# Hybrid encoder block, last stage: output blocks of three rows of experts, p's split in two pieces, u's split in two halves

## The chip, the cores and the metric

The kernel runs on one core of a Trainium2 chip. The metric is device time in microseconds of one execution. The core's engines are named as the profile names them: PE (matrix products; PEld is its weight load), DVE (vector), ACT (scalar and activation functions), POOL (GpSimd), SP (issues DMAs).

## What is computed

One layer: differential attention and a short convolution, merged by gates, then a retrieval over experts ("PEER") and a norm. All is float32 with S = D = 1024. Only the last part matters here:

```python
q = (xc @ w_query).reshape(c, PEER_HEADS, 2, PEER_HALF_DIM)
...
top, pos = lax.top_k(cand, PEER_TOPK)          # 8 heads x 16 experts a token
eidx = jnp.take_along_axis(cidx, pos, axis=-1)
g = jax.nn.softmax(top, axis=-1)
u = expert_u[eidx]
a = jax.nn.gelu(jnp.einsum('chkd,cd->chk', u, xc), approximate=False)
vv = expert_v[eidx]
return jnp.einsum('chk,chkd->cd', (g.astype(a.dtype) * a), vv)
```

There are 128 x 128 experts, each a row of 1024 values of u and one of v.

## The kernel before

The eight tiles of 128 tokens are treated in two ways. Five of them (NB = 5, GB = 640 tokens) are **dense**: every expert is computed for every token, and a table of weights w_d, zero where an expert wasn't chosen, selects. Three of them (NA = 3) are **gathered**: for each of the 128 chosen experts of a token, POOL fetches 128 rows of u and v at once (`gather_gen`, L727, the indirect DMA at L741), DVE forms the dot product (L748), ACT the gelu and the weight (L750, L751), and DVE accumulates (L761). Four slots (UVT) hold fetched rows; a fetch goes out when the accumulation four before it is done.

Both run together in the last stage (L890 to L1037). Its loop (L1000) goes over i, here called **step** i: one row of 128 experts of the 128 rows (NK).

- `expert_u(i+1)` (L926): the row's u arrives transposed, as 128 x 1024, by SP's DMA in one of three buffers `raw`. `split` (L903) makes two parts of it for products at full accuracy: ACT copies the high part (L906, tile uh), DVE subtracts it for the low part (L908, tile uhl).
- `expert_z(i)` (L930): 48 matmuls of 320 columns, z = hn u, in two halves of the tokens of 24 each; `expert_u(i+1)` stands between the halves. Then ACT's gelu makes p (L942, tile pr).
- `expert_p(i)` (L945): DVE multiplies p by the weights (L946), and `split` makes ph and phl of it. 
- `expert_v(i)` (L950): v's row is loaded into `raw` and split into vh and vhl.
- `expert_out` (L962): the output, 5 tiles of tokens x 2 halves of 512 columns, is formed for a **block** of BLK = 2 rows at a time, in as many parts as the block has rows, one part a step. Four of the ten output tiles ("held", r0 to r3) stay in PSUM to the end; for the six others ("moving", m0 to m5) PE writes `pout`, of which there are two buffers, and DVE adds it into hacc (L975). The order is m0 r0 m1 r1 m2 | r2 m3 r3 m4 m5. Each tile takes 3 matmuls for each row of the block. The block before the present one is put out: step i = 2b+2 and 2b+3 put out rows 2b and 2b+1. `after`, that is `expert_p` of step i, is called at the second tile.

The buffers of a kind are counted by PHB = 4 (ph, phl), VHB = 3 (vh, vhl), and 2 for uh and uhl. A tile takes the place of the oldest of its kind, when all instructions that use that one are done.

**What sets the order.** PE and DVE run in the order of the source in this stage (`manual_schedule`, L898). ACT, POOL and SP are ordered by a planner. The gather and the selection of experts (`select_gen`, L594; for the gathered tiles, `done` is given) are generators that `tick` (L148) steps on: each group of matmuls reports its time in us (L917: columns / 2400 x 3 x number of operands), 12.8 us a step in all, and a generator moves on when its own interval has gone by. The gather's is 2.36 us while the selection runs, and 1.78 us afterwards (GATHER, L1003), with one dot product or one accumulation at a time; the selection's is 13 us (SEL_STEP_D). What they put on DVE stands in DVE's order at that place.

```python
1014              made.append(expert_z(i, us.pop(0), ahead))
1015          if b >= 0:
1016              expert_out(pv[:BLK], vv[:BLK], part, b == 0, b == NK // BLK - 1, product)
1017          product()
1018          if b >= 0 and part == BLK - 1:
1019              pv, vv = pv[BLK:], vv[BLK:]
1020          if i < NK:
1021              vv.append(expert_v(i))
```

Of the kernel before, what the change touches and what calls it, by code (L numbers as in the profile page):

```python
# [20 lines left out]
P = 128  # L21
S = 1024
D = 1024
# [21 lines left out]
UVT = 4  # L45
PHB = 4
VHB = 3
BLK = 2
NR = 2
WB = 4  # L50
WT = 32
# [3 lines left out]
SEL_STEP = 1.5  # L55
SEL_STEP_D = 13
W_STEP = 1.6
# [8 lines left out]
def block_kernel(ctx, tc, x, wqkv, wcols, wpr, wo, wq, skT, uv, uT, an_w, fn_w, fin_w, sub_w,  # L66
# [527 lines left out]
    def select_gen(small, tt, ev, gw, done=None):  # L594
# [6 lines left out]
        for a in range(2):  # L601
# [23 lines left out]
            for j in range(2):  # L625
# [5 lines left out]
                else:  # L631
# [6 lines left out]
                                op=ALU.is_equal)  # L638
                PL.tensor_tensor(out=oh, in0=oh, in1=sfv[:, :, j, :].unsqueeze(3).broadcast_to(sh), op=ALU.mult)
                V.tensor_reduce(out=ev[j][:, a * 64:(a + 1) * 64].rearrange("p (h k) -> p h k", k=TOPK),  # L640
                                in_=oh.rearrange("p h a k -> p h k a"), axis=AX.X, op=ALU.add)
# [284 lines left out]
    def expert_u(i):  # L926
        u = split(raw_rows(uT[i]), "uh", 2, [P, D], V)
        return [(u[0][:, k * P:(k + 1) * P], u[1][:, k * P:(k + 1) * P]) for k in range(KD)]

    def expert_z(i, us, mid):  # L930
        b = i // WB
        if i % WB == 0:
            wts[b] = dn.tile([P, GB // WT, WB, WT], F32, name="wt", tag="wt", bufs=2)
            SP.dma_start(out=wts[b], in_=w_d[:, :, i:i + WB, :].rearrange("c p i t -> p c i t"))
        hs = halves(GB)
        z = ps_z.tile([P, 2, 512], F32, name="z", tag="z")[:, :len(hs), :hs[0][1]]
        for j, (c0, cn) in enumerate(hs):
            passes(z[:, j, :], us, [(hh[:, k, c0:c0 + cn], hl[:, k, c0:c0 + cn]) for k in range(KD)], cn)
            if j == 0:
                mid()  # L940
        p = dn.tile([P, GB], F32, name="pr", tag="pr", bufs=1)
        A.activation(p.rearrange("p (h c) -> p h c", h=len(hs)), z, AF.Gelu)  # L942
        return p

    def expert_p(i, p):  # L945
        V.tensor_mul(p.rearrange("p (c t) -> p c t", t=WT), p.rearrange("p (c t) -> p c t", t=WT),  # L946
                     wts[i // WB][:, :, i % WB, :])
        return split(p, "ph", PHB, [P, GB], V)

# [12 lines left out]
    def expert_out(pv, vv, part, first, last, after):  # L962
        n = len(order) // BLK
        for j, (t, hf) in enumerate(order[part * n:(part + 1) * n]):
            if j == 1:
                after()
# [10 lines left out]
    def finish_rows():  # L977
# [3 lines left out]
        for t in range(NB):  # L981
# [5 lines left out]
            else:  # L987
                y = hacc[:, t - NR, :]
            A.activation(du.tile([P, D], F32R, name="uh", tag="uh", bufs=2), y, AF.Square, accum_out=ss[:, t:t + 1])
            ys.append(y)  # L990
# [7 lines left out]

    pv, vv, us = [], [], [expert_u(0)]
    for i in range(NK + BLK):  # L1000
        b, part = i // BLK - 1, i % BLK
        made = []
        gather[2] = GATHER[sel not in gens]  # L1003

        def ahead():
            if i + 1 < NK:
                us.append(expert_u(i + 1))

        def product():
            if made:  # L1010
                pv.append(expert_p(i, made.pop()))

        if i < NK:
            made.append(expert_z(i, us.pop(0), ahead))
        if b >= 0:
            expert_out(pv[:BLK], vv[:BLK], part, b == 0, b == NK // BLK - 1, product)
        product()
        if b >= 0 and part == BLK - 1:
            pv, vv = pv[BLK:], vv[BLK:]
        if i < NK:  # L1020
            vv.append(expert_v(i))
        if i == 1:
            for t in range(NR, NB):
                SP.dma_start(out=hacc[:, t - NR, :], in_=h_d[t * P:(t + 1) * P, :])
# [66 lines left out]
```

## Time and profile before

| | |
|---|---|
| median of 3 runs | 3399.04 us (3398.12 to 3399.4) |
| the profiled execution | 3390.54 us, span 3388.8 us |
| mean granted TensorE clock | 0.959 of full speed |
| busy share of the span: PE, PEld, DVE, ACT, POOL | 91%, 83%, 78%, 38%, 26% |
| last stage: first and last product of z | 1315.3 and 3343.2 us |

The span is from the first to the last instruction. A busy time counts the time in which at least one instruction of the engine runs. PE's instructions overlap, so a busy PE isn't PE at its peak. "Idle before" is the time that the engine stood still just ahead of an instruction, and "<-" names what ended it. A window's clock is the share of the full TensorE clock that was granted, 2.4 GHz being 1.00 and 1.2 GHz 0.50.

### The profile page before, as it was taken

What the parts mean: (1) busy time and instruction counts of PE and PEld (TensorE: products, weight loads), DVE (VectorE), ACT (ScalarE), POOL (GpSimd) and SP (SyncE); (2) the same over time, 40 slices, a digit from 0 to 9 for tenths busy, and PEclk for the clock granted to TensorE, in tenths of its full rate; (3) what the DMA queues carried; (4) which work ended last, traced back from release to release, by engine and by line L of the source; (5) the groups of instructions that cost most, each with busy time, mean ns of one, the idle gap of its engine ahead of it and who ended that gap; (6) DMA issues with size and microseconds to landing.
All of it is one profiled execution on the core that took longest, in us unless ns stands there. A gap on an engine that the chain in (4) does not pass through costs nothing.

```text
span 3388.8 us, 45651 instructions
## 1 busy us (share of the span) xinstructions
PE 3073.1 (91%) x17551; PEld 2804.0 (83%) x17551; DVE 2659.0 (78%) x4661; ACT 1295.8 (38%) x2341; POOL 889.2 (26%) x712
## 2 busy tenths in 40 slices
PE   8999999898989887998998998998999988999896
PEld 6799988798988787887887887887888877888785
DVE  4442564589999965988898987888988888888888
ACT  3322462446577674323223323323223332333232
POOL 2310000154353542222222222222222322223232
PEclk9999999899999998999999998999999998999999
DMA  4442223735443656777787877787777888898886
GB/s 172 156 152 73 85 87 118 248 127 212 162 176 145 230 217 240 279 268 268 273 291 262 286 267 254 278 285 254 285 282 248 325 308 303 324 324 329 293 323 247
DMA packets 237547, 801.09 MB, mean 236 GB/s; under 512 B 18832, under 2 KB 123280, under 8 KB 174096
## 3 DMA queue, kind: packets, MB, share of 16 engines
q0 software_dynamic: 64704, 442.53, 35.3%
q1 hardware_dynamic: 152592, 305.30, 26.5%
q10 hardware_dynamic: 20032, 50.34, 3.9%
q8 instruction: 138, 2.26, 0.3%
q14 instruction: 81, 0.66, 0.1%
HBM read 714.74 MB, written 83.36 MB: 236 GB/s over the span
## 4 chain that ended last, share of the span: by engine, by line
PE 26%; issue 24%; DVE 22%; DMA 11%; POOL 9%; ACT 7%; SPq 0%; POOLq 0%; ACTq 0%; DVEq 0%
POOL uvt L741 8%; DMA raw<-in_uT 6%; PE pg L228 4%; DVE acc L761 3%; DVE uvt L748 3%; PE pq L228 3%; PE z L915 3%; PE ph L228 2%; DVE hacc L975 2%; PE py L228 2%; DVE vhl L908 2%; PE pout L915 2%; PE pw L694 2%; DVE phl L908 1%; DMA uvt<-in_uv,idx 1%
## 5 line engine op out<-in xcount | busy, mean ns | idle before, releaser
L741 POOL DMA_INDIRECT uvt<-in_uv,idx x384 | 498.4, 1298 | 1498.3 <-DVE acc L761 1447.3
L915 PE MATMUL z<-actTh,uhl 128*128 128x320 f32 x2048 | 645.1, 315 | 13.6 <-DVE uhl L908 13.6
L915 PE MATMUL z<-actTh,uh 128*128 128x320 f32 x2048 | 647.4, 316 | 7.7 <-ACT pr L942 5.8
L915 PE MATMUL z<-actTl,uh 128*128 128x320 f32 x2048 | 645.5, 315 | 0.0
L748 DVE SCALAR_TENSOR_TENSOR uvt<-uvt,hng 128x1024 f32<-128x1024 f32 x384 | 467.5, 1217 | 54.2 <-DMA uvt<-in_uv,idx 26.9
L761 DVE SCALAR_TENSOR_TENSOR acc<-uvt,wt,acc 128x1024 f32<-128x1024 f32 x384 | 490.7, 1278 | 5.3 <-DMA acc<-h_d 5.0
L915 PE MATMUL pout<-vh,ph 128*128 128x512 f32 x768 | 319.0, 415 | 175.9 <-DVE hacc L975 175.8
L915 PEld LDWEIGHTS z<-actTh,uh 128*128 128x128 f32 x2048 | 398.4, 195 | 15.4 <-ACT pr L942 6.7
L915 PEld LDWEIGHTS z<-actTh,uhl 128*128 128x128 f32 x2048 | 396.8, 194 | 14.0 <-DVE uhl L908 14.0
L915 PEld LDWEIGHTS z<-actTl,uh 128*128 128x128 f32 x2048 | 397.6, 194 | 6.6
L750 ACT ACTIVATE wt<-zt 128x1 f32<-128x1 f32 x384 | 77.0, 201 | 721.3 <-DVE uvt L748 721.0
L915 PEld LDWEIGHTS pout<-vh,ph 128*128 128x128 f32 x768 | 149.0, 194 | 231.8 <-DVE hacc L975 204.5
L915 PE MATMUL pout<-vhl,ph 128*128 128x512 f32 x768 | 311.7, 406 | 1.6 <-DVE vhl L908 1.6
L915 PE MATMUL pout<-vh,phl 128*128 128x512 f32 x768 | 311.6, 406 | 0.0
L975 DVE TENSOR_TENSOR hacc<-pout,hacc 128x512 f32<-128x512 f32 x384 | 262.2, 685 | 28.9 <-PE pout L915 27.9
L717 POOL TENSOR_TENSOR o<-ms,wtr 128x512 f32<-128x512 bf16 x160 | 204.5, 1322 | 255.0 <-PE pw L694 132.4
L185 DVE TENSOR_TENSOR wl<-wr,wh 128x2048 fp32r<-128x2048 f32 x66 | 157.9, 2393 | 113.9 <-ACT wh L184 113.9
L906 ACT CAST uh<-raw 128x1024 fp32r<-128x1024 f32 x128 | 134.7, 1052 | 280.1 <-DMA raw<-in_uT 226.0
L908 DVE TENSOR_TENSOR phl<-pr,ph 128x640 fp32r<-128x640 f32 x128 | 105.6, 825 | 152.6 <-ACT ph L906 151.0
L694 PE MATMUL pw<-o,o 128*128 128x128 f32 x1280 | 172.4, 288 | 39.5 <-POOL o L717 19.1
L184 ACT CAST wh<-wr 128x2048 fp32r<-128x2048 f32 x74 | 141.0, 1907 | 164.4 <-DMA wr<-in_wq 33.2
L694 PEld LDWEIGHTS pw<-o,o 128*128 128x128 f32 x1280 | 164.2, 202 | 47.6 <-POOL o L717 24.0
(290 smaller groups left out, 6831.2 us busy)
## 6 DMA issues: line engine op xcount, KB each, us to landing
raw<-in_uT SPq DMA_DIRECT2D x128, 512.0 KB
raw<-in_uv SPq DMA_DIRECT2D x128, 512.0 KB
w_d<-wbuf ACTq DMA_DIRECT2D x20, 2048.0 KB
wt<-w_d SPq DMA_DIRECT2D x32, 1280.0 KB
wr<-in_wcols SPq DMA_DIRECT2D x28, 1024.0 KB
wr<-in_wq SPq DMA_DIRECT2D x24, 1024.0 KB
xt<-in_x SPq DMA_DIRECT2D x16, 512.0 KB
q_d<-qt POOLq DMA_DIRECT2D x32, 256.0 KB
```

The lines of the kernel that those rows point to most:

```text
L184: A.copy(out=op[0][sl], in_=src)
L185: lo.tensor_sub(op[1][sl], src, op[0][sl].bitcast(F32))
L228: PE.matmul(pd, lhsT=l[a], rhs=r[b], start=i == 0 and j == 0, stop=i == n - 1 and j == len(c) - 1)
L694: PE.matmul(pw[:, u, :], lhsT=o2[:, t + u, :], rhs=o1[:, t + u, :], start=True, stop=True)
L717: PL.tensor_tensor(out=o1.rearrange("p t i -> p i t"), in0=ms[:, 0], in1=w[:, ts].unsqueeze(1).broadcast_to(sh), op=ALU.mult)
L741: PL.indirect_dma_start(out=t[:], out_offset=None, in_=uv, in_offset=bass.IndirectOffsetOnAxis(ap=sels[c][1][:, k:k + 1], axis=0))
L748: V.scalar_tensor_tensor(u, u, 1.0, st[c], op0=ALU.mult, op1=ALU.mult, accum_out=zt)
L761: V.scalar_tensor_tensor(acc, t[:, D:2 * D], wt, acc, op0=ALU.mult, op1=ALU.add)
L906: A.copy(out=hi, in_=t)
L908: eng.tensor_sub(lo, t, hi.bitcast(F32))
L915: PE.matmul(ps, lhsT=lhs[k][a], rhs=rhs[k][b], start=first and k == 0 and j == 0, stop=last and k == n - 1 and j == 2)
L975: V.tensor_add(hacc[:, t - NR, ds], ps, hacc[:, t - NR, ds])
```

## The change

Blocks of three rows in place of two (BLK), with 5 buffers for ph and phl, 4 for vh and vhl, 3 of half the size for uh and uhl, and weights loaded for three rows at a time. Tiles are put out as m0 r0 m1 r1 | m2 r2 m3 | r3 m4 m5; the last of the 43 blocks has two rows. The split of p: product and ACT's copy at the second tile of a step's output, the subtraction at the third. The split of u: its first half after the products that use the first half of u, the second after the others; z is now formed over the halves of u, for both halves of the tokens. The selection has one more halt, between POOL's product and DVE's sum (L639, L640), and an interval of 11.6 us. The last norm's scratch tile is of another kind.

```diff
@@ -43,17 +43,17 @@
 NE = PH * TOPK
 
 UVT = 4
-PHB = 4
-VHB = 3
-BLK = 2
+PHB = 5
+VHB = 4
+BLK = 3
 NR = 2
-WB = 4
+WB = 3
 WT = 32
 WQ = 4
 WFB = 2
 GATHER = (2.36, 1.78)
 SEL_STEP = 1.5
-SEL_STEP_D = 13
+SEL_STEP_D = 11.6
 W_STEP = 1.6
 MIXW = 3
 ATT = (5, 4)
@@ -637,6 +637,8 @@
                 V.tensor_tensor(out=oh, in0=pf.unsqueeze(2).broadcast_to(sh), in1=iota_k.unsqueeze(1).broadcast_to(sh),
                                 op=ALU.is_equal)
                 PL.tensor_tensor(out=oh, in0=oh, in1=sfv[:, :, j, :].unsqueeze(3).broadcast_to(sh), op=ALU.mult)
+                if done:
+                    yield
                 V.tensor_reduce(out=ev[j][:, a * 64:(a + 1) * 64].rearrange("p (h k) -> p h k", k=TOPK),
                                 in_=oh.rearrange("p h a k -> p h k a"), axis=AX.X, op=ALU.add)
                 yield
@@ -924,20 +926,26 @@
         return t
 
     def expert_u(i):
-        u = split(raw_rows(uT[i]), "uh", 2, [P, D], V)
-        return [(u[0][:, k * P:(k + 1) * P], u[1][:, k * P:(k + 1) * P]) for k in range(KD)]
+        ur = raw_rows(uT[i])
+        for h in range(2):
+            u = split(ur[:, h * 512:(h + 1) * 512], "uh", 3, [P, 512], V)
+            us[i].append([(u[0][:, k * P:(k + 1) * P], u[1][:, k * P:(k + 1) * P]) for k in range(KD // 2)])
+            yield
 
     def expert_z(i, us, mid):
         b = i // WB
         if i % WB == 0:
             wts[b] = dn.tile([P, GB // WT, WB, WT], F32, name="wt", tag="wt", bufs=2)
-            SP.dma_start(out=wts[b], in_=w_d[:, :, i:i + WB, :].rearrange("c p i t -> p c i t"))
+            n = min(WB, NK - i)
+            SP.dma_start(out=wts[b][:, :, :n, :], in_=w_d[:, :, i:i + n, :].rearrange("c p i t -> p c i t"))
         hs = halves(GB)
         z = ps_z.tile([P, 2, 512], F32, name="z", tag="z")[:, :len(hs), :hs[0][1]]
-        for j, (c0, cn) in enumerate(hs):
-            passes(z[:, j, :], us, [(hh[:, k, c0:c0 + cn], hl[:, k, c0:c0 + cn]) for k in range(KD)], cn)
-            if j == 0:
-                mid()
+        kh = KD // 2
+        for h in range(2):
+            for j, (c0, cn) in enumerate(hs):
+                xs = [(hh[:, k, c0:c0 + cn], hl[:, k, c0:c0 + cn]) for k in range(h * kh, h * kh + kh)]
+                passes(z[:, j, :], us[h], xs, cn, h == 0, h == 1)
+            mid()
         p = dn.tile([P, GB], F32, name="pr", tag="pr", bufs=1)
         A.activation(p.rearrange("p (h c) -> p h c", h=len(hs)), z, AF.Gelu)
         return p
@@ -945,7 +953,14 @@
     def expert_p(i, p):
         V.tensor_mul(p.rearrange("p (c t) -> p c t", t=WT), p.rearrange("p (c t) -> p c t", t=WT),
                      wts[i // WB][:, :, i % WB, :])
-        return split(p, "ph", PHB, [P, GB], V)
+        hi = dv.tile([P, GB], F32R, name="ph", tag="ph", bufs=PHB)
+        A.copy(out=hi, in_=p)
+        return p, hi
+
+    def expert_lo(p, hi):
+        lo = dv.tile([P, GB], F32R, name="phl", tag="phl", bufs=PHB)
+        V.tensor_sub(lo, p, hi.bitcast(F32))
+        return hi, lo
 
     def expert_v(i):
         vr = raw_rows(uv[i * P:(i + 1) * P, D:])
@@ -960,9 +975,9 @@
                 order.append(q.pop(0))
 
     def expert_out(pv, vv, part, first, last, after):
-        n = len(order) // BLK
-        for j, (t, hf) in enumerate(order[part * n:(part + 1) * n]):
-            if j == 1:
+        cut = [-(-len(order) * j // BLK) for j in range(BLK + 1)]
+        for j, (t, hf) in enumerate(order[cut[part]:cut[part + 1]]):
+            if j in (1, 2):
                 after()
             ds = slice(hf * 512, (hf + 1) * 512)
             lhs = [(p[0][:, t * P:(t + 1) * P], p[1][:, t * P:(t + 1) * P]) for p in pv]
@@ -986,7 +1001,7 @@
                     V.tensor_add(y[:, ds], held[t][hf], y[:, ds])
             else:
                 y = hacc[:, t - NR, :]
-            A.activation(du.tile([P, D], F32R, name="uh", tag="uh", bufs=2), y, AF.Square, accum_out=ss[:, t:t + 1])
+            A.activation(dv.tile([P, D], F32R, name="vh", tag="vh", bufs=VHB), y, AF.Square, accum_out=ss[:, t:t + 1])
             ys.append(y)
         yield
         r = rstd_of(ss, D, NB, "f")
@@ -996,25 +1011,32 @@
             SP.dma_start(out=out[t * P:(t + 1) * P, :], in_=ys[t])
             yield
 
-    pv, vv, us = [], [], [expert_u(0)]
-    for i in range(NK + BLK):
+    pv, vv, us = [], [], {0: []}
+    run(expert_u(0))
+    blocks = -(-NK // BLK)
+    for i in range((blocks + 1) * BLK):
         b, part = i // BLK - 1, i % BLK
         made = []
         gather[2] = GATHER[sel not in gens]
 
+        us[i + 1] = []
+        coming = expert_u(i + 1) if i + 1 < NK else iter(())
+
         def ahead():
-            if i + 1 < NK:
-                us.append(expert_u(i + 1))
+            next(coming, None)
 
         def product():
-            if made:
-                pv.append(expert_p(i, made.pop()))
+            if made and isinstance(made[0], tuple):
+                pv.append(expert_lo(*made.pop()))
+            elif made:
+                made[0] = expert_p(i, made[0])
 
         if i < NK:
-            made.append(expert_z(i, us.pop(0), ahead))
+            made.append(expert_z(i, us.pop(i), ahead))
         if b >= 0:
-            expert_out(pv[:BLK], vv[:BLK], part, b == 0, b == NK // BLK - 1, product)
-        product()
+            expert_out(pv[:BLK], vv[:BLK], part, b == 0, b == blocks - 1, product)
+        while made:
+            product()
         if b >= 0 and part == BLK - 1:
             pv, vv = pv[BLK:], vv[BLK:]
         if i < NK:
```

## Rows read from the trace of the kernel before


**Rows 1.** Windows: length; busy of PE, PEld, DVE, ACT, POOL; clock; DMA share; GB/s.

```profile
1400.00:2550.00 1150.00, 1061.36 (x5728) 955.54 (x5727) 998.29 (x1638) 349.56 (x703) 269.87 (x208) 0.96 0.77 273
2570.00:3340.00 770.00, 686.90 (x3699) 617.93 (x3699) 665.93 (x845) 238.21 (x523) 222.78 (x168) 0.96 0.86 311
```

**Rows 2.** The groups of instructions, PE, 1400 to 2550 us.

```profile
L915 PE MATMUL z<-actTh,uh 128*128 128x320 f32 x1179 | 372.3, 316 | 2.0 <-ACT pr L942 2.0
```

**Rows 3.** The groups of instructions, PE, 2570 to 3340 us.

```profile
L915 PE MATMUL z<-actTh,uh 128*128 128x320 f32 x761 | 239.4, 315 | 0.0
```

**Rows 4.** The timeline, all engines, 2902 to 2915 us (start, duration, instruction).

```profile
2902.39 0.31 PE L915 MATMUL z<-actTh,uh 128*128 128x320 f32 x1
...
2905.96 0.33 SPq L923 DMA_DIRECT2D raw<-in_uT  x1
...
2909.47 0.40 PE L915 MATMUL pout<-vh,ph 128*128 128x512 f32 x1
...
2914.35 1.05 ACT L906 CAST uh<-raw 128x1024 fp32r<-128x1024 f32 x1 [3.97 <-DMA raw<-in_uT]
...
2914.70 0.39 PE L915 MATMUL held<-vh,phl 128*128 128x512 f32 x1
```

**Rows 5.** The waits, 1400 to 2550 us (us in total, times, longest).

```profile
PE pout L915 <- DVE hacc L975: 86.6, 37, 12.1
...
DVE phl L908 <- ACT ph L906: 78.3, 71, 3.3
...
DVE hacc L975 <- PE pout L915: 18.0, 20, 2.7
DVE pr L946 <- ACT pr L942: 17.0, 10, 5.5
DVE e L640 <- POOL sc L639: 16.6, 8, 2.1
```

**Rows 6.** The waits, 2570 to 3340 us.

```profile
DVE phl L908 <- ACT ph L906: 63.9, 47, 8.2
...
DVE uvt L748 <- DMA uvt<-in_uv,idx: 20.6, 26, 2.0
```

**Rows 7.** The timeline, DVE alone, 2881 to 2890 us.

```profile
2881.60 0.82 DVE L946 TENSOR_TENSOR pr<-pr,wt 128x640 f32<-128x640 f32 x1
2883.21 0.83 DVE L908 TENSOR_TENSOR phl<-pr,ph 128x640 fp32r<-128x640 f32 x1 [0.79 <-ACT ph L906]
2883.95 1.28 DVE L761 SCALAR_TENSOR_TENSOR acc<-uvt,wt,acc 128x1024 f32<-128x1024 f32 x1
...
2886.29 0.69 DVE L975 TENSOR_TENSOR hacc<-pout,hacc 128x512 f32<-128x512 f32 x1
2886.89 1.27 DVE L761 SCALAR_TENSOR_TENSOR acc<-uvt,wt,acc 128x1024 f32<-128x1024 f32 x1
...
2888.69 1.22 DVE L908 TENSOR_TENSOR vhl<-raw,vh 128x1024 fp32r<-128x1024 f32 x1
2889.82 1.22 DVE L748 SCALAR_TENSOR_TENSOR uvt<-uvt,hng 128x1024 f32<-128x1024 f32 x1
```

**Rows 8.** The page, the costliest groups, the whole span.

```profile
L975 DVE TENSOR_TENSOR hacc<-pout,hacc 128x512 f32<-128x512 f32 x384 | 262.2, 685 | 28.9 <-PE pout L915 27.9
```

**Rows 9.** The page, the DMA issues, the whole span.

```profile
wt<-w_d SPq DMA_DIRECT2D x32, 1280.0 KB
```

**Rows 10.** The timeline, all engines, around 2003 us.

```profile
2002.55 0.40 PE L915 MATMUL pout<-vh,phl 128*128 128x512 f32 x1
...
2002.98 1.05 ACT L906 CAST vh<-raw 128x1024 fp32r<-128x1024 f32 x1 [4.00 <-PE pout L915]
...
2005.38 1.22 DVE L908 TENSOR_TENSOR vhl<-raw,vh 128x1024 fp32r<-128x1024 f32 x1
```

**Rows 11.** The windows, a wait of PE and what follows it.

```profile
2226.00:2230.70 4.70, 0.02 (x1) 0.00 (x0) 2.83 (x5) 1.96 (x4) 0.37 (x1) 1.00 0.82 295
2230.70:2235.00 4.30, 4.28 (x15) 3.71 (x16) 4.20 (x12) 2.39 (x4) 0.57 (x1) 0.60 0.79 266
```

## The prediction

> **What bounds the kernel now.** The change touches the last stage alone, the loop over 128 rows of experts ("steps"), so I read that stage by itself. The busy table of two stretches comes first [rows 1]: one in which the selection still runs (1400 to 2550 us) and one after it (2570 to 3340 us). DVE is busy 998.3 of 1150 us and 665.9 of 770 us, and no engine is full. A step has 16 products of each kind into z, so the counts give the steps: 1179 / 16 = 73.7 in the first stretch, 15.6 us each, and 761 / 16 = 47.6 in the second, 16.2 us each [rows 2, 3]. Products alone need less: in an undisturbed round the 48 products of z take 7.08 us (2902.39 to 2909.47) and 23 output products 5.23 us (to the start of the one at 2914.70), 0.2275 us each, so 30 take 6.8 us and a step 13.9 us [rows 4]. PE's one large wait is for DVE's addition into hacc, 86.6 us in the first stretch [rows 5].
>
> DVE works 998.3 / 73.7 = 13.55 us a step and idles 2.06. Over half of its idle time has one cause: phl waits for ACT's copy ph, 78.3 of 151.7 us, and 63.9 of 104.1 us in the second stretch [rows 5, 6]. DVE, in source order, therefore sets the pace, and PE follows it through two output buffers.
>
> **The change part by part.** Durations are taken from start to next start of queued DVE instructions [rows 7]: addition into hacc 0.60, p's subtraction 0.74, a whole row of v or u 1.13, p's product 0.82 (0.74 if something is queued behind it).
>
> Output blocks of three: the 384 additions [rows 8] become 43 x 6 = 258. That is 2 a step where 3 stood, 0.60 us of DVE a step. The number of matmuls stays the same; each output tile now has 9 in place of 6. Of the two output buffers, each is now freed a whole z earlier than PE wants it again, or nearly, so PE's wait for hacc goes.
>
> p's split: ACT's copy (0.79 us of DVE's idle time in the quiet case [rows 7]) lies under the gather steps of one output tile. The 1.06 us a step go; if no gather step falls between, 0.79 stays. The extra halt in the selection takes away the wait of e for POOL, 16.6 us in all [rows 5].
>
> u in halves: between 640 elements (0.74) and 1024 (1.13), a line through both gives 0.61 for 512, so 1.23 a step against 1.13: +0.10 (bounds 0, if the time follows the elements alone, and 0.35, if a half costs as much as 640 elements). ACT copies twice as often in smaller pieces and is two thirds idle. No copy moves onto the path.
>
> Weight loads of three rows: 43 loads in place of 32 [rows 9], the same bytes, in runs of 384 bytes in place of 512. The DMA share is 0.77 and 0.86 [rows 1], so I take nothing. If that cover were gone, DVE's wait for gathered rows would grow from the 20.6 us that it has now [rows 6]. The Trainium skill, "DMA: Bandwidth & Descriptors", Specifications, says that pieces below 512 bytes cost a read besides the write. By it these 42 MB would count twice, at 273 GB/s an estimated 154 us over a stage of 2030 us, so 0.86 becomes 0.94. No run here shows it, and the sum by it would stay the same unless the gather falls behind.
>
> **A new wait.** With these parts alone DVE would want 13.55 + 1.0 - 0.6 + 0.1 = 14.05 us a step, PE 13.9. But the buffers must be counted. A block's three rows of v and p are read until the last tile of its third output step. Call the steps that run the output of one block A, B, C. At the end of B, v of the block (three), of A and of B are live: five, and VHB is 4. p made in C is the sixth, and PHB is 5. So the split of v at the end of B must wait until the last tile m5 of C has read the oldest row. DVE stands in source order, so everything behind it waits too: the gather's dots and accumulations, u for the next step, the additions of C. In the kernel before, three v for blocks of two are enough: the copy vh is let go at 2002.98 by a product that started at 2002.55, and DVE comes to vhl only at 2005.38 [rows 10].
>
> The loop that closes through this wait, from m5's start S in C. DVE's other work is 13.55 - 5.63 = 7.92 us for 12.8 us of ticks, 0.62 per us. DVE: third product ended S+0.95, copy vh 1.05 (S+2.0), split 1.13, gather steps of half a z (3.2 us of ticks) 2.0, first half of u 0.61 and its end: S+5.8. PE stopped at the third product of z at S+2.3: a gap of 3.5 us. It runs 46 products of z and 7 of the next output tile, to S+14.2, where it needs vhl of C. DVE's way there: half a z 2.0, second half of u 0.61, three tiles' gather steps 3.6, p's product and subtraction 1.5, two additions 1.2, the split 1.13: S+15.8. A second gap of 1.6 us. Then nothing holds PE: 2 products, three tiles, z, three tiles, z, two tiles = 0.45 + 6.1 + 7.1 + 6.1 + 7.1 + 4.1 = 31.0. The block takes 46.8 us. DVE has 39.2 us of work in it and reaches the wait some 6 us early, so its delays in A and B are absorbed. Its delays in C are not. Of the present idle time, the waits for ph, for PE's output, for pr and for the selection fall away (DVE is late there, or the halt removes them): 151.7 - 78.3 - 18.0 - 17.0 - 16.6 = 21.8 us [rows 5] remain, 0.9 a block, and a third of the block is exposed: +0.3. So 47.1 us, **15.7 a step**. In the second stretch DVE works 14.0 a step, 0.65 per us of ticks; the 12.2 us of ticks in C add 0.4: 47.5 us, **15.8 a step**.
>
> The loads stand up to this: one issued at 2905.96 is copied at 2914.35 [rows 4], 8.4 us. The next u that takes the place of the late v can be issued at S+3.1, and DVE wants it at about S+17.7. SP's queue holds nothing else that is needed sooner, and POOL's next gathers go out as soon as DVE frees a slot; the four in flight land during DVE's wait.
>
> Sum: 80 steps x (+0.1) + 48 x (16.2 - 15.8 = -0.4) = 8 - 18 = **-10 us**. The start and the end change places: one more step without output at the start, some 6 us more output after the last z. The profiled execution took 3390.5 us (span 3388.8), 8.5 under the median of 3399.0; I put the difference on the median: **3389 us**.
>
> **Rivals.** *The wait decides nothing.* If DVE lagged PE by a step, the buffer would be free when DVE comes to it. Then the parts count in full: 14.1 and 14.4 us a step, 80 x 1.5 + 48 x 1.8 = 206 us less, 3193 us; with half of that lost again, 3296. Against it: PE's last tiles need additions that DVE makes just ahead of the wait, so DVE cannot come much later than PE.
>
> *The slack is worth more.* DVE reaches the wait 6 us early in each block, and the long stalls of now (12.1 us the longest of PE's for hacc [rows 5]) are then hidden; with that the step falls to PE's chain with half its gaps, (41.7 + 2.5) / 3 = 14.7 to 15.4 us: 3300 to 3365.
>
> *Slower: the gap brings the clock down where nothing hides it.* After 4.7 us with PE at 0.02 us of work the granted clock was 0.60 over the next 4.3 us [rows 11], that is mostly at 1.2 GHz; 0.40 x 4.3 = 1.7 us lost. The new gap of 3.5 us comes once a block. In my sum the products behind it have 1.6 us until vhl, which covers the loss. If the clock falls at the second gap as well, or later, 43 x 1.7 = 73 us come on top: 3462 us. It decides if the half-clock stretch reaches past S+14. The Trainium skill, "TensorE: Matmul & The Clock Gate", HAM oscillation, tells of a loop that waits in every round and comes back at half clock each time; the rows agree that a wait is followed by that, and by the page alone the sum would be the 3462.
>
> *The split does not come apart.* Where no gather step falls between product and subtraction, 0.79 us stay. DVE has 6 us to spare in two steps of three, so this costs at most 43 x 0.8 = 34 us: 3423.
>
> **How the numbers follow.** About 0.2% (7 us) is what a measurement of this kernel can tell from no change. The wait as summed: 0.48, own range 3365 to 3415 (u's bounds, 0.25 us x 43 steps C, on one side; a third of the exposed idle time on the other); of it 0.26 ends below 3392, 0.10 within 7 us of 3399, 0.12 above. The wait decides nothing: 0.14, faster. The slack is worth more: 0.14, faster. Slower by the clock or by the split: 0.24. So faster 0.54, same 0.10, slower 0.36. The range 3305 to 3455 leaves out most of the first rival and the top of the clock's, together under 0.2.
>
> **What would show it.** Right: DVE waits some 6 to 7 us once in three steps ahead of vhl, for ACT's vh, which waits for PE's pout; PE waits for uhl about 3.5 us once in three steps, and no longer for hacc; phl no longer waits; hacc x258; the step is 15.7 us in both stretches. Wrong: vhl without such a wait and a step near 14.3; or PE's clock below 0.95 over long stretches and a step above 16.

## The result, and the profile of the changed kernel

The changed kernel takes 3451.5 us (median of 4 runs, 3448.7 to 3465.0) against 3399.2 us, a ratio of 1.0162 with a 95% interval of [1.0135, 1.0189]: slower by 1.6%, where 3389 us was forecast. The time lies inside the stated range of 3305 to 3455 us, at its upper end; the direction is the other one. The profiled execution took 3452.0 us with a span of 3450.2.

The windows and waits show the mechanism of the forecast, at another size. First the windows of the same two stretches (columns as in [rows 1]):

```profile
1400.00:2550.00 1150.00, 1046.85 (x5560) 947.01 (x5560) 936.30 (x1591) 356.51 (x756) 252.24 (x201) 0.96 0.75 264
2570.00:3340.00 770.00, 683.08 (x3589) 614.16 (x3589) 622.47 (x828) 238.10 (x550) 204.31 (x162) 0.95 0.83 301
```

DVE does less in the same time than before (936 against 998 us, 622 against 666), and PE a little less. The waits of the first stretch, then of the second (us in total, times, longest):

```profile
DVE vhl L910 <- ACT vh L908: 175.0, 24, 11.0
...
PE z L917 <- DVE uhl L910: 86.9, 28, 5.5
...
DVE phl L962 <- ACT ph L957: 28.9, 20, 5.6
...
PE pout L917 <- DVE vhl L910: 13.8, 14, 3.2
```

```profile
ACT uh L908 <- DMA raw<-in_uT: 111.8, 35, 11.9
...
PE z L917 <- DVE uhl L910: 74.3, 26, 4.7
DVE vhl L910 <- ACT vh L908: 57.9, 15, 6.4
DVE phl L962 <- ACT ph L957: 50.8, 16, 6.6
...
ACT vh L908 <- DMA raw<-in_uv: 39.4, 16, 6.1
...
PE pout L917 <- DVE vhl L910: 9.8, 9, 2.3
```

Among DVE's waits a new one stands at the top: vhl for vh, once a block, 42 times in all. PE's wait for hacc [rows 5] is gone but for 0.5 and 2.6 us, and in its place PE waits for u's half. The costliest groups of the whole span count the same things:

```profile
L917 PE MATMUL z<-actTh,uhl 128*128 128x320 f32 x2048 | 676.0, 330 | 183.1 <-DVE uhl L910 183.1
...
L990 DVE TENSOR_TENSOR hacc<-pout,hacc 128x512 f32<-128x512 f32 x258 | 176.1, 683 | 3.0 <-PE pout L917 2.9
...
L910 DVE TENSOR_TENSOR vhl<-raw,vh 128x1024 fp32r<-128x1024 f32 x128 | 157.7, 1232 | 244.1 <-ACT vh L908 244.1
```

258 additions in place of 384 [rows 8], and 244.1 us of DVE's idle time ahead of vhl, 5.8 us a block.

One such wait in the timeline of DVE, then the copy on ACT that it waits for, then PE:

```profile
2018.53 0.69 DVE L990 TENSOR_TENSOR hacc<-pout,hacc 128x512 f32<-128x512 f32 x1
2027.55 1.23 DVE L910 TENSOR_TENSOR vhl<-raw,vh 128x1024 fp32r<-128x1024 f32 x1 [8.33 <-ACT vh L908]
...
2030.19 1.27 DVE L763 SCALAR_TENSOR_TENSOR acc<-uvt,wt,acc 128x1024 f32<-128x1024 f32 x1
2031.37 1.22 DVE L750 SCALAR_TENSOR_TENSOR uvt<-uvt,hng 128x1024 f32<-128x1024 f32 x1
...
2032.51 0.68 DVE L910 TENSOR_TENSOR uhl<-raw,uh 128x512 fp32r<-128x512 f32 x1
```

```profile
2026.46 2.00 ACT L908 CAST vh<-raw 128x1024 fp32r<-128x1024 f32 x2 [4.07 <-PE pout L917]
```

```profile
2033.25 0.64 PE L917 MATMUL z<-actTh,uhl 128*128 128x320 f32 x1 [5.17 <-DVE uhl L910]
```

DVE is done with its addition at 2019.2 and stands for 8.33 us until PE lets go of the oldest row and ACT has copied into its place. Between vhl and uhl lie one step of the selection and two gather instructions, 3.8 us, where the forecast had the mean of 2.0. PE waits 5.17 us, where it had 3.5. This is one of the dear blocks: over the 40 blocks counted below, the work between vhl and uhl is 1.1 to 3.9 us and its mean 2.0, the forecast's figure.

Four blocks, from one vhl behind the wait to the next (the second figure is the length, the third PE's busy time):

```profile
1596.60:1646.73 50.13, 45.69 (x236) 40.72 (x235) 37.66 (x66) 17.04 (x35) 10.49 (x8) 0.93 0.73 251
1790.42:1837.18 46.76, 43.90 (x236) 39.67 (x235) 39.66 (x59) 14.25 (x32) 11.93 (x9) 0.96 0.76 268
1980.41:2027.55 47.14, 42.59 (x236) 38.14 (x235) 37.61 (x65) 14.66 (x32) 9.62 (x8) 1.00 0.73 266
2808.67:2865.61 56.94, 48.14 (x236) 43.09 (x235) 39.12 (x52) 16.36 (x38) 12.92 (x10) 0.88 0.80 282
```

The shortest blocks last 46.8 us, the length of the forecast's chain; in them 1.2 us of work lies between vhl and uhl. The mean is 48.3 us over the 24 blocks from 1404 to 2563 us (16.1 a step) and 50.2 over the 16 from there to 3366 (16.7 a step), against forecasts of 47.1 and 47.5.

Where the rest lies shows when each block is cut at two points: the start of vhl of C (the last row of the block), and the start of PE's first product that reads it, m0's eighth. Means in us, from the timelines of DVE and PE:

| part of a block | forecast | first stretch | second stretch |
|---|---|---|---|
| DVE's way through C, from vhl of B to vhl of C | 12.7, second stretch 13.1 | 13.2 | 13.1 |
| from there to PE's first product with vhl of C | 1.1 | 1.8 | 1.5 |
| PE's way from that product to the next vhl of B | 33.0 | 33.3 | 35.6 |

DVE's way is nearly as forecast. The last part is 33.0 to 33.2 us in 20 of the 24 blocks of the first stretch, but in 11 of the 16 blocks of the second stretch PE waits there for uhl, 0.4 to 4.0 us (in 2 blocks of the first, under 1 us). One such wait, by the timelines of SP's queue, ACT, DVE and PE:

```profile
3024.65 0.38 SPq L940 DMA_DIRECT2D wt<-w_d  x1
3030.10 3.12 SPq L925 DMA_DIRECT2D raw<-in_uT  x1
```

```profile
3043.49 0.62 ACT L908 CAST uh<-raw 128x512 fp32r<-128x512 f32 x1 [5.97 <-DMA raw<-in_uT]
...
3044.21 0.71 ACT L957 CAST ph<-pr 128x640 fp32r<-128x640 f32 x1
```

```profile
3044.95 0.82 DVE L962 TENSOR_TENSOR phl<-pr,ph 128x640 fp32r<-128x640 f32 x1 [3.42 <-ACT ph L957]
...
3052.11 0.68 DVE L910 TENSOR_TENSOR uhl<-raw,uh 128x512 fp32r<-128x512 f32 x1
```

```profile
3052.85 0.41 PE L917 MATMUL z<-actTh,uhl 128*128 128x320 f32 x1 [2.34 <-DVE uhl L910]
```

A row of u that was issued behind a load of weights is late on ACT, ACT's copy ph stands behind it, DVE stands for ph, and PE, two products into the next z, stands for uhl. DVE still waits 4.32 us for vh at the end of this block: it had time to spare, and PE had not.

### The profile page after: what moved, and what is told of

The parts are those of the page before. It is cut to its first block, busy times and chain, and to the rows that moved or that the text cites. A ratio compares the mean times of both kernels' runs of the same rounds, so it can differ in the third digit from the quotient of the medians.

```text
span 3450.2 us, 45896 instructions
## 1 busy us (share of the span) xinstructions
PE 3105.3 (90%) x17551; PEld 2838.2 (82%) x17551; DVE 2598.0 (75%) x4663; ACT 1321.0 (38%) x2469; POOL 868.6 (25%) x712
## 3 DMA queue, kind: packets, MB, share of 16 engines
q1 hardware_dynamic: 180928, 305.30, 26.6%
q8 instruction: 138, 2.26, 0.3%
## 4 chain that ended last, share of the span: by engine, by line
PE 46%; issue 19%; DVE 17%; POOL 6%; DMA 6%; ACT 5%; SPq 0%; POOLq 0%; DVEq 0%; ACTq 0%
PE z L917 13%; PE pout L917 7%; PE held L917 6%; POOL uvt L743 6%; PE pg L228 4%; PE pq L228 3%; PE ph L228 2%; DVE uvt L750 2%; DVE acc L763 2%; PE py L228 2%; DVE vhl L910 2%; PE pw L696 1%; PE pv L228 1%; DMA wr<-in_wq 1%; DMA raw<-in_uT 1%
## 5 line engine op out<-in xcount | busy, mean ns | idle before, releaser
L743 POOL DMA_INDIRECT uvt<-in_uv,idx x384 | 467.4, 1217 | 1572.2 <-DVE acc L763 1489.0
L917 PE MATMUL z<-actTh,uhl 128*128 128x320 f32 x2048 | 676.0, 330 | 183.1 <-DVE uhl L910 183.1
L917 PE MATMUL z<-actTh,uh 128*128 128x320 f32 x2048 | 667.2, 326 | 8.2 <-ACT pr L950 6.6
L917 PE MATMUL z<-actTl,uh 128*128 128x320 f32 x2048 | 664.8, 325 | 0.0
L917 PEld LDWEIGHTS z<-actTh,uhl 128*128 128x128 f32 x2048 | 416.3, 203 | 198.9 <-DVE uhl L910 198.9
L917 PEld LDWEIGHTS z<-actTh,uh 128*128 128x128 f32 x2048 | 415.7, 203 | 14.0 <-ACT pr L950 7.4
L910 DVE TENSOR_TENSOR vhl<-raw,vh 128x1024 fp32r<-128x1024 f32 x128 | 157.7, 1232 | 244.1 <-ACT vh L908 244.1
L908 ACT CAST uh<-raw 128x512 fp32r<-128x512 f32 x256 | 157.1, 618 | 374.7 <-DMA raw<-in_uT 247.1
L908 ACT CAST vh<-raw 128x1024 fp32r<-128x1024 f32 x128 | 130.2, 1049 | 256.4 <-PE pout L917 150.6
L917 PE MATMUL held<-vhl,ph 128*128 128x512 f32 x512 | 201.8, 394 | 0.0
## 6 DMA issues: line engine op xcount, KB each, us to landing
wt<-w_d SPq DMA_DIRECT2D x42, 960.0 KB, 11.8
```

What stands on the lines that cost most here:

```text
L743: PL.indirect_dma_start(out=t[:], out_offset=None, in_=uv, in_offset=bass.IndirectOffsetOnAxis(ap=sels[c][1][:, k:k + 1], axis=0))
L908: A.copy(out=hi, in_=t)
L910: eng.tensor_sub(lo, t, hi.bitcast(F32))
L917: PE.matmul(ps, lhsT=lhs[k][a], rhs=rhs[k][b], start=first and k == 0 and j == 0, stop=last and k == n - 1 and j == 2)
```

## Experiments

All ratios are against the kernel before, which took 3398 to 3402 us beside them. My theory: DVE's wait for the oldest row of v sets the block. Rivals: the other parts cost it (u in halves, smaller weight loads), or the clock does.

**The wait taken away without a buffer.** v of step B is split behind C's last tile, and so is p of C:

```diff
-            if j in (1, 2):
+            if j in (1, 2) and not (part == BLK - 1 and not last):
                 after()
...
-        while made:
-            product()
         if b >= 0 and part == BLK - 1:
             pv, vv = pv[BLK:], vv[BLK:]
-        if i < NK:
-            vv.append(expert_v(i))
+            late = [j for j in (i - 1, i) if j < NK]
+        else:
+            late = [i] if i < NK and (b < 0 or part != BLK - 2) else []
+        for j in late[:1]:
+            product()
+            vv.append(expert_v(j))
+        while made:
+            product()
+        for j in late[1:]:
+            vv.append(expert_v(j))
```

> The changed kernel; in the last step C of a block DVE now makes v of step B, the split of p of C and v of C only behind the last output tile, in that order; no buffer is added. Theory (DVE waits for the oldest row of v at the end of B and stands still for a third of C): the wait of vhl for ACT's vh falls from 244 us to under 40, PE's waits for uhl from 183 us to under 60, the shortest block from 46.8 us to 43 to 44.5, and the time to 3180 to 3270 us, most likely 3210. Rival (the parts of the change themselves cost it: u in halves, weight loads in 384-byte runs, or the clock): these are untouched, so the time stays at 3420 to 3480.

Measured: 3213.5 us, 0.9463 [0.9429, 0.9496]. Its first stretch in the windows, and its vhl and z in the groups of the whole span:

```profile
1400.00:2550.00 1150.00, 1143.97 (x6394) 1044.98 (x6393) 1070.45 (x1781) 404.41 (x869) 302.49 (x234) 1.00 0.86 304
```

```profile
L917 PE MATMUL z<-actTh,uhl 128*128 128x320 f32 x2048 | 638.4, 312 | 17.8 <-DVE uhl L910 17.7
...
L910 DVE TENSOR_TENSOR vhl<-raw,vh 128x1024 fp32r<-128x1024 f32 x128 | 157.6, 1231 | 0.0
```

244 us of waiting become 0.0, PE's 183 become 17.7, PE is busy 1144 of 1150 us and the granted clock is 1.00. The same instructions in another order are 238 us faster than the changed kernel. The theory stands.

**The wait taken away by a buffer:**

```diff
-VHB = 4
+VHB = 5
-WB = 3
+WB = 2
...
-            u = split(ur[:, h * 512:(h + 1) * 512], "uh", 3, [P, 512], V)
+            u = split(ur[:, h * 512:(h + 1) * 512], "uh", 2, [P, 512], V)
```

> The changed kernel with a fifth buffer of v; its room comes from weight loads of two rows (256-byte runs) and two in place of three buffers of u's halves. Theory (the missing fifth buffer sets the block): no wait of vhl for vh ahead of C's tiles; what is left is phl of C, which waits for the last tile because p has five buffers for six rows, some 3 us a block with the gather steps behind it; 3200 to 3320 us, most likely 3260. Rival (small loads and u in halves cost the time): it stays at 3450 or rises, as the loads get smaller still and u's halves have one buffer less.

Measured: 3218.2 us, 0.9481 [0.9448, 0.9513], the theory again: vhl waits 0.0 here too, and 42 us better than expected.

**Everything but the longer block:**

```diff
-PHB = 5
-VHB = 4
-BLK = 3
+PHB = 4
+VHB = 3
+BLK = 2
```

> The changed kernel with blocks of two, four buffers of p and three of v as in the kernel before; the split of p apart, u in halves, the halt in the selection and weight loads of three rows stay. Theory (only the longer block brings a wait): phl's waits of 78.3 and 63.9 us are mostly gone, u costs 0.1 us a step, 14.7 to 15.0 us a step in the first stretch and 15.3 to 15.5 in the second; 3260 to 3340 us, most likely 3285. Rival (u in halves at 0.35 us a step, small loads, or the clock make the change slow): 3399 or more.

Measured: 3256.9 us, 0.9590 [0.9555, 0.9626], 28 us better than expected. The other parts of the change are worth 142 us, and the step from blocks of two to blocks of three, with its one buffer each, loses 195. Without the wait the longer block is a gain: v made late, with blocks of three, is 43 us below this run.

**p's split apart, alone**, in the kernel before:

```diff
-        return split(p, "ph", PHB, [P, GB], V)
+        hi = dv.tile([P, GB], F32R, name="ph", tag="ph", bufs=PHB)
+        A.copy(out=hi, in_=p)
+        return p, hi
```

(with its subtraction one output tile later, as in the change)

> The kernel before with the split of p taken apart alone (its subtraction one output tile behind its product). Theory: the 142 us that phl waits for ph in the two stretches fall to under 30; if nothing takes their place 3257 us, most likely 3290, range 3260 to 3340. Against the run with blocks of two that has all other parts too it differs by under 20 us. Rival (this wait hides others, PE for its output buffers above all): 3370 to 3400.

Measured: 3338.4 us, 0.9824 [0.9792, 0.9856]. A gain of 60 us, at the poor end of the range; phl still waits 52.0 us for ph between 1400 and 2400 us (65.9 before), longest 8.9. Its longest wait, on ACT and then on DVE:

```profile
1701.57 1.05 ACT L906 CAST uh<-raw 128x1024 fp32r<-128x1024 f32 x1 [10.00 <-DMA raw<-in_uT]
...
1702.96 0.71 ACT L949 CAST ph<-pr 128x640 fp32r<-128x640 f32 x1
```

```profile
1703.70 0.82 DVE L954 TENSOR_TENSOR phl<-pr,ph 128x640 fp32r<-128x640 f32 x1 [8.90 <-ACT ph L949]
```

ACT's copy ph stands behind a copy of u whose row is late, and the split comes apart to no avail. The run lies 81 us above the one with all parts and blocks of two, where under 20 was expected: something in the change that I had priced near zero is worth most of it.

**Blocks of three, alone:**

```diff
-PHB = 4
-VHB = 3
-BLK = 2
-WB = 4
+PHB = 5
+VHB = 4
+BLK = 3
+WB = 2
```

> The kernel before with blocks of three alone (five buffers of p, four of v, as in the changed kernel; weight loads of two rows make the room); p's split and u stay as they were. Theory (the wait of v of step B sets the block): vhl waits for vh 4 to 10 us once in three steps, the shortest block is 46.8 plus some 0.8 us (phl waits for ACT's copy again, u's whole row comes 0.5 us later), the time 3465 to 3560 us, most likely 3490. Rival (the longer block costs nothing, the other parts do): 0.6 us of DVE a step less, so 3320 to 3395.

Measured: 3466.9 us, 1.0182 [1.0151, 1.0214]; vhl waits 219.3 us, 42 times, and the shortest block is 46.6 us. The theory's case, with the chain as long as in the changed kernel. The weight loads of two rows are part of this run too; against the kernel before with such loads alone (3343.8 us, below) the longer block costs 123 us.

**u in halves, alone** (the change's own expert_u, its loop in expert_z and the last norm's scratch tile, on the kernel before):

```diff
-        u = split(raw_rows(uT[i]), "uh", 2, [P, D], V)
...
+        for h in range(2):
+            u = split(ur[:, h * 512:(h + 1) * 512], "uh", 3, [P, 512], V)
```

> The kernel before with u in halves alone. The run with blocks of two and all other parts came out 81 us below the one with p's split apart alone; what lies between them is u in halves, the halt in the selection and the size of the weight loads. If u in halves gives it: 3320 to 3350 us. If it costs what the forecast took (0.1 us a step): 3399 to 3412, and the halt or the loads gave the 81.

Measured: 3419.7 us, 1.0053 [1.0031, 1.0076]: a cost of 17 to 20 us, near the forecast's 0.1 us x 128 = 13. It is not what the 81 us come from.

**The gap filled**, to see what the clock costs:

```diff
+        if i % BLK == 0 and i >= 2 * BLK:
+            for _ in range(16):
+                PE.matmul(z[:, 0, :], lhsT=hh[:, 0, 0:P], rhs=hh[:, 0, 0:hs[0][1]], start=True, stop=True)
```

> The changed kernel with 16 products more, into z's own buffer ahead of z, in the first step of each block (they lie where PE waits for u's first half, 2.4 us in place of idle time; z starts over behind them). If the time of a block over its shortest (46.8 us) comes from the clock: the granted clock rises from 0.955 to 0.98 or more, the blocks with two drops (48 to 50 us) fall to 47, and the time to 3380 to 3420. If DVE's loop sets the block by itself: the shortest block stays at 46.8 us and the time moves by under 15 us, 3436 to 3466.

Measured: 3442.8 us, 1.0109 [1.0065, 1.0152]. The granted clock rises to 0.98 in both stretches, and the shortest block stays at 46.7 us. PE's waits in the first stretch:

```profile
PE z L917 <- DVE uhl L910: 32.1, 25, 3.1
PE pout L917 <- DVE vhl L910: 26.0, 20, 2.9
```

PE waits less for uhl (86.9 before) and more for vhl of C (13.8 before; in the second stretch 26.6 in place of 9.8): what the clock gives back, PE spends waiting for DVE. The gain is 9 us by the medians and 18 by the two ratios, whose intervals meet. The clock drops as the forecast's rival had it, and DVE's loop sets the block all the same.

**Four raw buffers:**

```diff
-WB = 3
+WB = 2
-    t = du.tile([P, D], F32, name="raw", tag="raw", bufs=3)
+    t = du.tile([P, D], F32, name="raw", tag="raw", bufs=4)
```

> The changed kernel with four in place of three buffers of the rows as loaded (weight loads of two rows make the room). If late loads make the blocks of the second stretch longer than those of the first (50.2 against 48.3 us): ACT's waits for raw rows, 112 and 39 us there, fall below 50 together, and the time to 3400 to 3425. If they don't: 3445 to 3460.

Measured: 3406.0 us, 1.0007 [0.9992, 1.0023]. ACT's waits for raw rows in the second stretch are 28.6 and 18.3 us in place of 111.8 and 39.4. Late loads are a part of the excess, but two things were changed here, and the later run below puts most of it on the loads' size.

**What the 81 us are.** First u in halves together with p's split apart, that is the diffs of these two runs in one kernel:

```diff
+        hi = dv.tile([P, GB], F32R, name="ph", tag="ph", bufs=PHB)
...
+            u = split(ur[:, h * 512:(h + 1) * 512], "uh", 3, [P, 512], V)
```

> The kernel before with p's split apart and u in halves, without the halt in the selection and with loads of four rows. Alone, p's split apart gave 3338 us and u in halves 3420 (20 more than before); with the halt and loads of three rows both gave 3257. If u in halves pays once p's split no longer holds DVE: 3255 to 3275. If the halt (or the loads) gave it: 3335 to 3365.

Measured: 3338.1 us, 0.9828 [0.9784, 0.9872]: u in halves adds nothing to p's split. Then p's split with the halt in the selection:

```diff
-SEL_STEP_D = 13
+SEL_STEP_D = 11.6
...
+                if done:
+                    yield
```

> The kernel before with p's split apart and the halt in the selection between POOL's product and DVE's sum. If the halt gives the 81 us between the run with p apart alone and the run with blocks of two and all other parts: 3250 to 3275. If it takes away the 16.6 us that e waits for POOL and no more: 3318 to 3330. If the overlap of POOL and DVE costs as much as it saves: 3335 to 3345.

Measured: 3322.6 us, 0.9777 [0.9741, 0.9813]: the halt, with the shorter interval that comes with it, is worth 16 us. That it equals the 16.6 us of e's wait [rows 5] is in part luck: over the whole stage e waited 20.7 us and no longer waits, but DVE's instructions beside POOL's product take 11 us more (last section). What was left is the size of the weight loads: blocks of two and all other parts, with

```diff
-WB = 3
+WB = 4
```

> The run with blocks of two and all other parts, with weight loads of four rows (1280 KB) as before in place of three. If the size of the loads gave what is left of the 81 us (the halt gave 16, u in halves nothing): 3305 to 3330 us, ACT's wait for raw u in the first stretch back from 70 to over 120 us, phl's wait for ph from 16 to about 50. If u in halves and the halt together gave it: 3250 to 3265.

Measured: 3349.9 us, 0.9862 [0.9824, 0.9901], 93 us more than with loads of three rows, and beyond the range that I gave. ACT's wait for raw u between 1400 and 2400 us is 144.5 us again (69.6 with three), phl's for ph 58.6 (16.5). That is 27 us slower than p's split with the halt, and the one other part, u in halves, had added nothing to p's split: the parts do not add up, and no run shows why.

The kernel before, with loads of two rows alone:

```diff
-WB = 4
+WB = 2
```

> The kernel before with weight loads of two rows alone. If shorter loads let the rows of u come in time: phl's wait for ph falls from 66 us and PE's wait for hacc with it, 3330 to 3370 us. If pieces of 256 bytes cost a second access, or nothing changes: 3395 to 3450.

Measured: 3343.8 us, 0.9836 [0.9812, 0.9861]. One constant gives 55 us. ACT's wait for raw u between 1400 and 2400 us falls from 119.2 to 83.0. phl's wait in the first stretch did not fall as expected (65.9 to 63.8); PE's for hacc did in the second (73.1 to 57.6 us between 2570 and 3200, longest 11.6 to 7.3). And the changed kernel with loads of two rows:

```diff
-WB = 3
+WB = 2
```

> The changed kernel with weight loads of two rows (640 KB) alone; three raw buffers. If the size of the loads made the 45 us that the run with four raw buffers and loads of two rows gained: 3400 to 3415 us. If the fourth raw buffer did: 3440 to 3460.

Measured: 3415.6 us, 1.0047 [1.0027, 1.0066]: 36 of the 45 us of the run with four raw buffers are the loads, the fourth buffer gives 10.

The number of rows in a load also sets in which step of a block it falls. In the kernel before, loads of four and of two rows both fall in the first step, so its 55 us are the size's. With blocks of two, loads of three rows fall in either step by turns, and in the changed kernel so do loads of two; size and place were not told apart there.

How a load holds up a step shows in the kernel before too. SP's queue, then ACT, then DVE:

```profile
1437.23 0.38 SPq L934 DMA_DIRECT2D wt<-w_d  x1
1444.17 2.88 SPq L923 DMA_DIRECT2D raw<-in_uT  x1
```

```profile
1456.48 1.04 ACT L906 CAST uh<-raw 128x1024 fp32r<-128x1024 f32 x1 [9.06 <-DMA raw<-in_uT]
1457.43 0.70 ACT L942 ACTIVATE pr<-z 128x640 f32<-128x640 f32 x1
```

```profile
1458.16 0.82 DVE L946 TENSOR_TENSOR pr<-pr,wt 128x640 f32<-128x640 f32 x1 [5.54 <-ACT pr L942]
```

The row of u that is issued 6.9 us behind the 1280 KB load takes 2.88 us to issue (0.33 otherwise) and is copied 12.3 us after that began. ACT, in the order that the planner gave it, stands 9.06 us for it with pr behind it, and DVE waits for pr. Over these 20 us the DMA engines are full:

```profile
1437.00:1457.00 20.00, 18.49 (x97) 15.85 (x96) 14.32 (x25) 4.25 (x8) 4.59 (x4) 1.00 1.01 368
```

The packets of all queues, from 1438 to 1449 us and from there to 1458:

```profile
DMA packets 2687, 3.93 MB, mean 358 GB/s; under 512 B 45, under 2 KB 2352, under 8 KB 2352
```

```profile
DMA packets 845, 3.32 MB, mean 369 GB/s; under 512 B 76, under 2 KB 329, under 8 KB 582
```

The load comes in pieces of 512 bytes, a row in pieces of 4 KB, the gathers in pieces of 8 KB. From 1438 to 1449 us no piece of a row moves (2352 packets under 2 KB, and no more under 8 KB), afterwards 253 do. The Trainium skill, "DMA: Bandwidth & Descriptors", Queues, rings and completion order, says that each DMA engine takes the pieces of one queue in their order; these counts agree. How much of the row's 12.3 us is this order, and how much the gathers that share the engines, was not told apart: no run here moved the loads to another queue. The median from issue to landing is 15.3 us for loads of 1280 KB (blocks of two and all other parts), 11.8 for 960 KB (the changed kernel) and 9.6 for 640 KB (the kernel before with such loads).

**Late v with two-row loads and four raw buffers**, on the kernel with v of step B made late:

```diff
-WB = 3
+WB = 2
-    t = du.tile([P, D], F32, name="raw", tag="raw", bufs=3)
+    t = du.tile([P, D], F32, name="raw", tag="raw", bufs=4)
```

> The run with v of step B made late, with four in place of three buffers of the rows as loaded (weight loads of two rows make the room). In the first stretch PE is at 99 per cent there, so nothing is to be had; in the second it idles 5 per cent, part of it for late loads. Theory (late loads cost what is left): 3180 to 3200 us. Rival (POOL and DVE at the gather set the second stretch): 3205 to 3220.

Measured: 3218.4 us, 0.9467 [0.9428, 0.9505], the same as without. With DVE's wait gone and PE busy 1144.0 of 1150 us in the first stretch, late rows cost nothing that this run shows.

**The version to keep** is the one with v of step B made late: 3213 us, 5.4% under the kernel before.

## Why the prediction was wrong

*The wait, and its place: right.* vhl waits for vh once a block, 5.8 us on the mean where 6 to 7 were forecast; PE waits for uhl (183.1 us, 4.4 a block, where 3.5 were forecast) and hardly for hacc; the shortest blocks are 46.8 us; the additions are 258. phl was to wait no longer and still does, 28.9 and 50.8 us. The edits that take the wait away give 3213 and 3218 us, inside the 3193 to 3296 that the prediction gave to the rival in which the wait decides nothing.

*The step that failed is "Then nothing holds PE", and with it "its delays in A and B are absorbed" and "The loads stand up to this".* All that could come on top of the chain was priced in the last term of the block, "a third of the block is exposed: +0.3". Measured are +1.5 us a block in the first stretch and +3.4 in the second (48.3 and 50.2 against 46.8; I had +0.3 and +0.7). By steps this is 80 x (16.1 - 15.7) + 48 x (16.7 - 15.8) = 75 us, where the run missed by 62; the 13 us between lie in the first blocks and the end, which I have not divided. In the second stretch DVE's way through C is 13.1 us, as forecast, and 2.6 of the 3.4 us lie in the part where nothing was to hold PE: late rows of u delay DVE in A and B, and PE waits for uhl. DVE's spare time covers DVE, which still waits 2.6 us or more for vh in each of these blocks; it does not cover PE, which wants each half of u on time. Loads of two rows gave 36 us and the fourth raw buffer 10, and with both, that part is 33.1 us in the first stretch and 33.9 in the second. In the first stretch the 1.5 us are spread over all three parts: 0.5 on DVE's way (5.6 us of waiting for ph in one block, 2.2 and 2.6 for the selection in two others), 0.7 where PE comes late to vhl of C, 0.3 behind it. The gather work in the chain was sized right (2.0 us on the mean).

*"So I take nothing", for the weight loads, was wrong too, and to the other side.* It was bounded on the side of a loss alone. Going from four rows to three or two is a gain: 55 us in the kernel before with two, 93 with three in the kernel with blocks of two. So this error hides a part of the miss; the changed kernel with loads of four rows was not run. The stalls that the prediction let fall away with the other parts came in part from the loads: with two rows, DVE's wait for pr in the first stretch goes from 17.0 us [rows 5] to 10.0, and PE's for hacc as above.

Small pieces do cost something. SP's queue in the kernel before (pieces of 512 bytes), in the changed kernel (384) and in the kernel before with two-row loads (256), by the pages: packets, MB, time of the packets as a share of 16 engines' span:

```profile
q1 hardware_dynamic: 152592, 305.30, 26.5%
```

```profile
q1 hardware_dynamic: 180928, 305.30, 26.6%
```

```profile
q1 hardware_dynamic: 235024, 305.30, 28.3%
```

That is 898, 918 and 946 us of all 16 engines for the same bytes; over all runs 897 to 903, 908 to 923 and 943 to 966. By the Trainium skill's rule on pieces below 512 bytes, "DMA: Bandwidth & Descriptors", Specifications, the 42 MB would count twice, an estimated 124 us more (898 x 42 / 305). The runs show a cost, of about 10 to 20 us with 384 bytes and 45 to 65 with 256, short of that. The kernel with pieces of 256 bytes is the faster one all the same.

*p's split, u in halves, the halt:* p's split alone gave 60 us of the 142 that phl waits [rows 5, 6], as ACT's copy ph can stand behind a late copy of u (the 8.90 us above); the halt gave 16 (forecast 16.6, see there); u in halves cost 17 to 20 by itself (forecast 13).

*The clock.* The number of that rival, 3462 us, is nearest to the result, but that is luck: its mechanism is not the cause. The drops are there: PE's 236 matmuls of a block take 42.6 us at a granted 1.00, 43.9 at 0.96, 44.5 to 45.7 at 0.93 (half-clock stretches at 1.2 GHz among 2.4). They do not set the block: with the gap filled the clock stands at 0.98, the middle part of the table falls from 1.8 to 1.4 us and from 1.5 to 1.3, the last part rises from 33.3 to 33.8 in the first stretch, and the blocks last 48.5 and 50.0 us on the mean, against 48.3 and 50.2. That run gained 9 to 18 us where the rival had 73. The drops agree with the pattern in the Trainium skill, "TensorE: Matmul & The Clock Gate", HAM oscillation, a loop that comes back at half clock after each wait. The time that was worked out from it, 3462 us, is not borne out.

*The other rivals.* The sum of "the slack is worth more" does not come out: 14.7 to 15.4 us a step are 80 x (0.9 to 0.2) + 48 x (1.5 to 0.8) = 144 to 54 us less, 3255 to 3345 us and not 3300 to 3365. The result lies outside both.

*The sign.* The forecast of -10 us was the difference of two large terms: by its own sums the parts without the wait were worth 206 us and the wait cost 196. Measured, the parts without the wait are worth 186 us (3213 us), and the wait costs 238. The errors, 20 and 42 us, make up the miss of 62: small beside either term, and larger than what was left between them. 0.36 for slower was too little for such a difference.

## What to carry to other kernels

Count live buffers against the ring at each step of a longer block; where one is missing, look first for an order in which the wait falls where the engine has nothing urgent behind it, since that was worth as much as the buffer (3213 and 3218 us). Spare time ahead of a wait covers the engine that waits there and no other: DVE had some 6 us to spare in a block, and PE was held all the same when DVE was late in the steps between (2.6 us a block in the second stretch). Where a forecast is the small difference of two large terms, forecast each of them and give both signs their share. And price a large periodic load by what is queued behind it: halving it gave 55 us here, more than the 52 that the whole change cost.

## What the runs showed of the hardware

A DVE instruction can take three times as long beside POOL. With the halt, POOL's product is no longer waited for at once, and DVE goes on; in the timelines of POOL and DVE of the changed kernel:

```profile
2601.49 2.85 POOL L639 TENSOR_TENSOR sc<-sc,sf 128x1024 bf16<-128x1024 bf16 x1 [1.18 <-issue]
```

```profile
2601.28 1.28 DVE L763 SCALAR_TENSOR_TENSOR acc<-uvt,wt,acc 128x1024 f32<-128x1024 f32 x1
2602.47 2.42 DVE L910 TENSOR_TENSOR uhl<-raw,uh 128x512 fp32r<-128x512 f32 x1
```

The half row of u, 0.68 us elsewhere, starts 1 us behind POOL's product and ends 0.55 us after it. The selection makes ten such products between 1500 and 2650 us. Beside nine of them the DVE instruction that starts second and reads two tiles in SBUF is drawn out like this: it takes 1.95 to 2.96 us and ends 0.54 to 1.08 us after POOL's, a little less than it takes elsewhere (0.68 to 1.28). That is 14 us of DVE's time in all, and 11 us beside eight products in the run with p's split and the halt. DVE instructions that began ahead of POOL's product are not drawn out, nor is the addition into hacc, which reads pout in PSUM (0.68 us at 2096.31, inside the product of 2095.28). POOL's product takes 1.93 us in the kernel before, where DVE stands still for it, and 2.26 to 2.92 us here. The Trainium skill, "SBUF — State Buffer", SBUF: two separate sides, says that the two engines hold a shared pair of ports in turn, for a whole instruction, where DVE's has two inputs in SBUF; these cases agree. No run differs in this alone, so what it costs the kernel was not measured; the halt gains 16 us with it.
